# The first normed x by rows and transposes, the odd layer's bias laid out by the host, and the second x.T piece behind the first weights

## The chip, the cores and the metric

The kernel runs on one core of one Trainium2 chip. The metric is the device time of one execution in microseconds (us), lower is better. Five engines work beside each other and meet only at semaphores: TensorE (PE in the profile, with its weight loads as PEld), VectorE (DVE), ScalarE (ACT), GpSimd (POOL) and SyncE (SP). SP, ACT and POOL also issue DMA transfers. Each engine takes its instructions strictly in the order in which the kernel was written out, so an instruction that waits holds up everything behind it on the same engine.

## The reference

Three transformer blocks on 256 tokens of width 1024, all in float32. What matters here is the start of the first block and the neighbourhood attention of the second:

```python
def rmsnorm(x, g):
    y = xf * lax.rsqrt(jnp.mean(xf * xf, axis=-1, keepdims=True) + EPS)
    return y * g

# layer 0 (even)
h = rmsnorm(x, norm_gain[0])
qa, ka, va, qb, kb, vb, qm, gate = split_cols(h @ w_in_even, SPLIT_EVEN)
...
# layer 1 (odd): each of 16 heads, rows of 64 positions
dc = jnp.clip(col[None, :] - col[:, None] + NA_COLS - 1, 0, 2 * NA_COLS - 2)
rpb_cols = rpb[:, :, dc]
s = einsum('bqhd,bikhd->bhqik', qblk, kblk) * scale + bias
s = jnp.where(colmask[:, None, :], s, -jnp.inf)
p = jax.nn.softmax(s)
```

Before them the keys and values of a memory are projected, and after them come a third block (a dilated attention with a gated convolution, a cross attention, a squared-ReLU MLP) and a last norm. The bulk of the work is matrix products of the 256 tokens with about 32 million weights.

## The kernel before

**Numbers.** Every product is made at nearly float32 accuracy from float32r parts. A weight tile `raw` from HBM is split by `split` (lines 430 to 436) into a high part `wh`, written by ACT, and a low part `wl` = raw − wh, written by DVE. The activations have a high and a low part too (`hilo`, or ACT with a scale and DVE's `scalar_tensor_tensor` with the same scale). `mm3` (line 438) then makes high times high, high times low and low times high.

**The plan.** The kernel's methods do not issue instructions. `Plan.record` (line 83) writes each of them down with what it depends on, and `Plan.order` (line 162) runs a list schedule over a simple model of the five engines: at each moment the engine takes, of its ready instructions, the one with the lowest priority number, which is the place in the recording plus `nc.bias` plus `SHIFT`. Transfers are modelled as one bus after the other: 450 ns per issue on SP and ACT, or 1040 ns on POOL, 650 ns of latency, bytes at 358 per ns (line 227), and 950 ns until the data can be used. The sequence that comes out is what all engines' queues get. Semaphores then follow the real dependences between tiles, so a wrong guess of the model costs waiting and nothing else. `either` records an instruction that DVE or ACT may take, whichever is free first in the model; `scaled` and `square_sum` are such.

**Buffers.** `raw` has three buffers, `wh` and `wl` four each. Activations live in 24 equal slots (`slot`). PSUM has four banks under the name `mm` (projections) and four under `at` (attention, transposes).

**The start.** `consts` (line 368) loads the gains, then the first two of x.T's eight 128-row pieces (x.T is prepared by the host), one on SP's and one on ACT's queue, and has PE run 24 warm-up matmuls. `layer_even` (line 1008) begins with the columns of w_in that make q, k and v of the first attention and k and v of the second, 896 columns in all. It does not wait for the norm: `gain_t` (line 519) multiplies x.T by the gain per row into the tile `gh`, and the missing factor 1/rms of each token is applied to the products later. For each of the eight 128-row pieces k, `columns` issues the loads of the weights and `sweep` makes 12 matmuls of 512 and 384 columns into four PSUM banks. Between the loads of weights `load_x` issues the rest of x.T, two pieces at a time. With pieces 6 and 7 come the rows of x itself, from which `sums` and `rstd` get 1/rms (POOL makes the power).

**The first normed x** (lines 1059 to 1067). All later products of this layer need the normed and transposed x, tile `hT`. `spread` (line 534) turns the column r of 1/rms into a row by two diagonal matrices and two float32 matmuls with ones (four PE instructions), and ACT copies the result to SBUF. DVE multiplies x.T by gain and row, eight times 128x256 (tile `xs`), and `hilo` splits this in four pieces of 128x512. The odd layer does the same step in another way: `norm_later` scales x by rows (tile `xn`), and `turns` (line 657) transposes it on PE in 128x128 pieces, with the gain applied while ACT and DVE split the result out of PSUM (tile `mT`).

**The odd layer's bias** (lines 1169 to 1193). For each group of four heads POOL issues two loads of shifted table rows (`rpbraw`), then writes `rpbe`, the column mask minus the table read backwards, with one 128x384 subtraction per head. The bias therefore has the opposite sign, and so have the scores: `heads8` scales q by −0.125, and `softmax` (line 745) adds, takes the minimum, and exponentiates with scale −1.0. The dilated attention of the third block goes through the same code, with its bias in the constants `C_DIL`.

Of the kernel before, what the change touches and what calls it, by code (L numbers as in the profile page):

```python
# [16 lines left out]
P = 128  # L17
S = 256
# [8 lines left out]
C_ID, C_COS, C_SIN, C_DIL, C_COL, C_END = 0, 128, 256, 384, 640, 704  # L27


class Plan:  # L30
# [131 lines left out]
    def order(self, prio):  # L162
# [37 lines left out]
        while len(seq) < n:  # L200
# [19 lines left out]
            if o["bytes"]:  # L220
                if e != "gpsimd":
                    ring[e] = max(ring[e], t) + 450.0
                    avail[e] = (ring[e], i)
                    bus = max(bus, ring[e] + 650.0)
                else:
                    bus = max(bus, end[i] + 650.0)
                bus += o["bytes"] / 358.0
                done = bus + o["after"]
# [79 lines left out]
class Kernel:  # L308
# [59 lines left out]
    def consts(self):  # L368
# [12 lines left out]
        for k, queue in enumerate((nc.sync, nc.scalar)):  # L381
            self.load_x(k, 1, queue)
# [136 lines left out]
    def gain_t(self, src, key, fast=False):  # L519
# [4 lines left out]
        def turn(k):  # L524
            v, g, h, l = src[k // 4][:, k % 4, :], self.gcol(key, k), f(0, k), f(1, k)
            if k == 0 and fast:
# [218 lines left out]
    def softmax(self, sc, bias=None, sink=None, causal=False):  # L745


# [8 lines left out]
        else:  # L756
            for t in range(2):
                nc.vector.tensor_tensor_reduce(out=p[:, t, :n[t]], in0=sc[:, t, :n[t]], in1=bias[t], scale=1.0,
                                               scalar=-NEG if sink is None else NEG, op0=ALU.add,
                                               op1=ALU.min if sink is None else ALU.max, accum_out=nmax[:, t:t + 1])  # L760
# [247 lines left out]
    def layer_even(self):  # L1008
# [5 lines left out]
        def columns(k0, parts, raw=None):  # L1014
# [4 lines left out]
            for j0, j1, d0, d1 in parts:  # L1019
# [17 lines left out]
        for k0 in range(0, KT, 2):  # L1037
            raw = columns(k0, ((0, 1, 0, 512), (0, 2, 512, 768), (0, 2, 768, 896), (1, 2, 0, 512)) if k0 == 0 else
                          ((0, 2, 0, 768), (0, 2, 768, 896)) if k0 < 6 else ((0, 1, 0, 768), (0, 1, 768, 896)))
            if k0 < 6:  # L1040
                self.load_x(k0 + 2, 2, nc.sync)
            else:
# [16 lines left out]
        rb = self.spread(r, self.work("y", [P, S], YB))  # L1059
        hT = Halves(lambda: self.slot([P, 2, 2, S], "hT"))  # L1060
        for c in range(2):
            t = self.slot([P, 4, S], "xs", F32)
            for k in range(4):
                nc.vector.scalar_tensor_tensor(t[:, k, :], self.xT[c][:, k, :], self.gcol("norm0", 4 * c + k), rb,
                                               ALU.mult, ALU.mult)
            for k in (0, 2):
                self.hilo(*hT.pair(4 * c + k), t[:, k:k + 2])
# [70 lines left out]
    def heads8(self, tag, w_in, cq, ck, cv, hT, bias, out, causal=False, before=None):  # L1138

        qs, ks = [], []  # L1140
        for i in range(2):
            ks.append(self.k_stack(self.proj_t(w_in, ck + 256 * i, hT)))
            qs.append(self.q_stack(self.proj_t(w_in, cq + 256 * i, hT), -0.125))
# [11 lines left out]
    def layer_odd(self, ms):  # L1155
# [13 lines left out]
        col = self.c[:, C_COL:C_COL + 64]  # L1169
        rpb = a["rpb_c"]  # L1170

        def biases(gi):
            e = {}

            def bias(h):
                hh = 8 * gi + h
                if h % 4 == 0:
                    raw = self.slot([P, 4, 220], "rpbraw", F32)
                    for rl in range(2):
                        nc.gpsimd.dma_start(raw[rl * 64:(rl + 1) * 64],  # L1180
                                            bass.AP(rpb.tensor, rpb.offset + hh * 465 + 76 + 31 * rl,
                                                    [[1, 64], [465, 4], [1, 220]]))
                    for j in range(4):
                        if j % 2 == 0:
                            e[h + j] = self.slot([P, 2, 6, 64], "rpbe", F32)
                        e[h + j] = e[h + j - j % 2]
                        w = bass.AP(raw.tensor, raw.offset + 220 * j + 218, [list(raw.ap[0]), [-31, 6], [-1, 64]])
                        nc.gpsimd.tensor_tensor(e[h + j][:, j % 2], col.unsqueeze(1).to_broadcast([P, 6, 64]), w,
                                                ALU.subtract)
# [369 lines left out]
```

## Time and profile before

| | |
|---|---|
| time, median of 3 runs | 773.08 us (772.73 to 773.56) |
| the profiled execution's own time | 773.77 us |
| its span, first to last instruction | 771.9 us |
| granted TensorE clock, mean | 0.997 |
| ACT busy | 529.0 us (69%) |
| read from HBM | 134.92 MB, 176 GB/s over the span |
| DMA issued by SP and ACT (q1) | 131.12 MB, 52.7% of 16 engines |
| DMA issued by POOL (q0) | 8.10 MB, 4.8% of 16 engines |
| chain that ended last | PE 82%, ACT 6%, DVE 6%, DMA 3%, issue 2% |

How to read it: "busy" is the time in which an engine has an instruction under way. Matmuls overlap each other, so a busy PE may still be faster or slower than its peak. A row of a group gives the line, engine and operation, the tile written, the tiles read, the shape, the number of instructions, then total busy us and mean ns of one, and last the idle time just before them with what ended it. Almost all instructions have the line 284, since `Plan.issue` emits them; the tiles' names tell them apart. A row of the timeline begins with start and length in us, and merges neighbours of one kind (x2).

### The profile page before, as it was taken

The page shows a single profiled execution, that of the slowest core. Times are in us where ns is not written, and L with a number is a line of the kernel's source. Part 1 is how long each engine was busy: PE and PEld are TensorE (multiplying, and loading weights), DVE is VectorE, ACT ScalarE, POOL GpSimd, SP SyncE. Part 2 cuts the span into 40 slices and gives each one's busy share as a digit, 9 for nine tenths or more (in the row PEclk, how much of TensorE's full clock was granted, in tenths as well). Part 3 has the DMA queues.
Part 4 walks back from the last instruction along what each step waited for, and adds up shares of the span by engine and source line. Part 5 has one row for each costly group of instructions (what it writes and reads, how often), then busy time and mean ns, then how long its engine had stood idle before and what let it go on. Part 6 is the DMA issues. An engine that isn't in the chain of part 4 may idle for free.

```text
span 771.9 us, 11841 instructions
## 1 busy us (share of the span) xinstructions
PE 760.7 (99%) x4370; PEld 662.6 (86%) x4370; DVE 614.3 (80%) x1136; ACT 529.0 (69%) x1034; POOL 66.6 (9%) x98
## 2 busy tenths in 40 slices
PE   9999999999999999999999999999999999999996
PEld 7898888888888888888888898899988888888885
DVE  5999998988779789979998899886677665555655
ACT  5687986976678678757796788466556765555562
POOL 2140010000001511132001000100000000000000
PEclk9999999999999999999999999999999999999998
DMA  8893555445568854765456644356535665656541
GB/s 315 284 268 111 165 183 177 159 165 164 164 211 250 218 188 144 199 197 193 134 191 194 191 163 156 117 165 219 191 110 164 195 188 167 204 177 209 170 163 55
DMA packets 109145, 140.39 MB, mean 182 GB/s; under 512 B 3744, under 2 KB 80736, under 8 KB 109088
## 3 DMA queue, kind: packets, MB, share of 16 engines
q1 hardware_dynamic: 103184, 131.12, 52.7%
q0 software_dynamic: 5472, 8.10, 4.8%
q8 instruction: 34, 0.56, 0.3%
q10 hardware_dynamic: 432, 0.43, 0.2%
q14 instruction: 23, 0.19, 0.1%
HBM read 134.92 MB, written 1.05 MB: 176 GB/s over the span
## 4 chain that ended last, share of the span: by engine, by line
PE 82%; ACT 6%; DVE 6%; DMA 3%; issue 2%; SPq 0%; POOLq 0%; POOL 0%; ACTq 0%; DVEq 0%
PE t_mm L284 61%; PE t_at L284 21%; DVE t_wl L284 2%; DMA t_raw<-in_w_in_even_dram 2%; ACT t_p L284 2%; ACT t_wh L284 2%; ACT t_y L284 1%; DVE t_y L284 1%; DVE t_p L284 1%; DMA t_xT<-in_x_t_dram 0%; ACT t_ph L284 0%; SPq L284 0%; ACT t_sum L284 0%; DVE t_pl L284 0%; DVE t_tanh L284 0%
## 5 line engine op out<-in xcount | busy, mean ns | idle before, releaser
L284 DVE TENSOR_TENSOR t_wl<-t_raw,t_wh 128x1024 fp32r<-128x1024 f32 (+2 forms) x238 | 288.7, 1217 | 69.9 <-ACT t_wh L284 67.2
L284 ACT ACTIVATE t_wh<-t_raw 128x1024 fp32r<-128x1024 f32 (+2 forms) x238 | 249.7, 1054 | 78.7 <-PE t_mm L284 57.4
L284 PE MATMUL t_mm<-t_mT,t_wh 128*128 128x512 f32 x496 | 179.6, 401 | 0.0
L284 PE MATMUL t_mm<-t_mT,t_wl 128*128 128x256 f32 x496 | 131.0, 283 | 0.0
L284 PE MATMUL t_mm<-t_wh,t_yh 128*128 128x512 f32 (+1 forms) x288 | 113.3, 393 | 0.0
L284 PE MATMUL t_mm<-t_wl,t_yh 128*128 128x512 f32 (+1 forms) x288 | 112.3, 390 | 0.0
L284 PE MATMUL t_mm<-t_wh,t_yl 128*128 128x512 f32 (+1 forms) x288 | 111.9, 391 | 0.0
L284 PEld LDWEIGHTS t_mm<-t_mT,t_wh 128*128 128x128 f32 x496 | 91.0, 188 | 13.4
L284 PEld LDWEIGHTS t_mm<-t_mT,t_wl 128*128 128x128 f32 x496 | 93.2, 189 | 6.6
L284 PE MATMUL t_at<-t_mT,t_wh 128*128 128x512 f32 x240 | 86.0, 395 | 0.0
L284 ACT COPY t_sum<-t_mm 128x256 f32<-128x256 f32 x90 | 33.2, 369 | 51.8 <-PE t_mm L284 51.3
L284 PE MATMUL t_mm<-t_wh,t_gh 128*128 128x256 f32 (+2 forms) x256 | 63.8, 333 | 0.0
L284 PEld LDWEIGHTS t_mm<-t_wl,t_yh 128*128 128x128 f32 x288 | 54.2, 188 | 10.7
L284 PEld LDWEIGHTS t_mm<-t_wh,t_yl 128*128 128x128 f32 x288 | 54.1, 188 | 10.6
L284 PEld LDWEIGHTS t_mm<-t_wh,t_yh 128*128 128x128 f32 x288 | 54.1, 188 | 10.3 <-ACT t_yh L284 0.3
L284 PE MATMUL t_at<-t_mT,t_wl 128*128 128x256 f32 x240 | 62.6, 280 | 0.0
L284 ACT ACTIVATE t_p<-t_p,t_st 128x256 f32<-128x256 f32 (+1 forms) x111 | 53.2, 494 | 10.6 <-DVE t_st L284 10.5
L284 PEld LDWEIGHTS t_at<-t_mT,t_wh 128*128 128x128 f32 x240 | 44.5, 188 | 8.3 <-issue 0.2
L284 DVE TENSOR_TENSOR t_sum<-t_mm,t_sum 128x256 f32<-128x256 f32 x90 | 37.9, 422 | 13.9 <-ACT t_sum L284 12.9
L284 PE MATMUL t_mm<-t_hT,t_wh 128*128 128x512 f32 (+1 forms) x160 | 48.3, 356 | 0.0
L284 PEld LDWEIGHTS t_at<-t_mT,t_wl 128*128 128x128 f32 x240 | 45.2, 188 | 3.5
L284 PE MATMUL t_mm<-t_gh,t_wh 128*128 128x512 f32 x128 | 47.3, 404 | 0.0
(189 smaller groups left out, 1371.7 us busy)
## 6 DMA issues: line engine op xcount, KB each, us to landing
t_raw<-in_w_in_odd_dram SPq DMA_DIRECT2D x20, 1024.0 KB, 5.2
t_raw<-in_w_up_dram SPq DMA_DIRECT2D x16, 1024.0 KB, 5.7
t_raw<-in_w_down_dram SPq DMA_DIRECT2D x16, 1024.0 KB, 5.0
t_raw<-in_w_in_dram SPq DMA_DIRECT2D x12, 1024.0 KB, 5.3
t_raw<-in_w_in_even_dram SPq DMA_DIRECT2D x10, 1024.0 KB, 5.1
t_raw<-in_w_mem_kv_dram SPq DMA_DIRECT2D x8, 1024.0 KB, 5.2
t_raw<-in_w_out_even_dram SPq DMA_DIRECT2D x6, 1024.0 KB, 5.2
t_raw<-in_w_out_odd_dram SPq DMA_DIRECT2D x6, 1024.0 KB, 5.9
```

Of the source, the lines that this page charges most:

```text
L284: f(*[self.real(v) for v in args], **{k: self.real(v) for k, v in kwargs.items()})
```

## The change

- The second x.T piece goes from ACT's queue to SP's, behind the first three loads of weights (`columns` now also takes pieces of x.T in its list). Rows 2 and 3 of the weights come as two loads of 384 KB instead of one of 768 KB, with the last 128 columns of both between them.
- In `gain_t` DVE makes the high part of the second x.T piece too, which ACT made before.
- The planner's model moves bytes at 320 per ns instead of 358.
- The first normed x is made as in the odd layer: four scalings of x by rows (`xn`), 16 transposes on PE, and eight halves each on ACT and DVE.
- The host lays out the odd layer's bias per head as 128x384 with mask and sign in it; POOL loads two heads at a time (384 KB) and computes nothing. Scores keep their sign: q is scaled by 0.125, and in `softmax` the sum is negated by the scale of the same DVE instruction. The bias of the dilated attention changes sign in the constants, and the column mask leaves them.

```diff
@@ Plan.order
-                bus += o["bytes"] / 358.0
+                bus += o["bytes"] / 320.0
@@ consts
-        for k, queue in enumerate((nc.sync, nc.scalar)):
-            self.load_x(k, 1, queue)
+        self.load_x(0, 1, nc.sync)
@@ gain_t
-            if k == 0 and fast:
+            if k < 2 and fast:
                 nc.vector.tensor_scalar(h, v, g, None, ALU.mult)
@@ softmax
-                nc.vector.tensor_tensor_reduce(out=p[:, t, :n[t]], in0=sc[:, t, :n[t]], in1=bias[t], scale=1.0,
-                                               scalar=-NEG if sink is None else NEG, op0=ALU.add,
-                                               op1=ALU.min if sink is None else ALU.max, accum_out=nmax[:, t:t + 1])
+                nc.vector.tensor_tensor_reduce(out=p[:, t, :n[t]], in0=sc[:, t, :n[t]], in1=bias[t], scale=1.0 if sink else -1.0,
+                                               scalar=NEG if sink else -NEG, op0=ALU.add,
+                                               op1=ALU.max if sink else ALU.min, accum_out=nmax[:, t:t + 1])
@@ layer_even, columns
-            for j0, j1, d0, d1 in parts:
+            for part in parts:
+                if len(part) == 2:
+                    self.load_x(*part, nc.sync)
+                    continue
+                j0, j1, d0, d1 = part
@@ layer_even, the loop over k0
-            raw = columns(k0, ((0, 1, 0, 512), (0, 2, 512, 768), (0, 2, 768, 896), (1, 2, 0, 512)) if k0 == 0 else
-                          ((0, 2, 0, 768), (0, 2, 768, 896)) if k0 < 6 else ((0, 1, 0, 768), (0, 1, 768, 896)))
-            if k0 < 6:
-                self.load_x(k0 + 2, 2, nc.sync)
-            else:
+            raw = columns(k0, (((0, 1, 0, 512), (0, 2, 512, 768), (0, 2, 768, 896), (1, 1), (1, 2, 0, 512), (2, 2)),
+                               ((0, 1, 0, 768), (0, 2, 768, 896), (1, 2, 0, 768), (4, 2)),
+                               ((0, 2, 0, 768), (0, 2, 768, 896), (6, 2)),
+                               ((0, 1, 0, 768), (0, 1, 768, 896)))[k0 // 2])
+            if k0 == 6:
@@ layer_even, the normed x
-        rb = self.spread(r, self.work("y", [P, S], YB))
-        hT = Halves(lambda: self.slot([P, 2, 2, S], "hT"))
+        halves = [self.slot([P, 2, 512], "xn", F32) for _ in range(2)]
         for c in range(2):
-            t = self.slot([P, 4, S], "xs", F32)
-            for k in range(4):
-                nc.vector.scalar_tensor_tensor(t[:, k, :], self.xT[c][:, k, :], self.gcol("norm0", 4 * c + k), rb,
-                                               ALU.mult, ALU.mult)
-            for k in (0, 2):
-                self.hilo(*hT.pair(4 * c + k), t[:, k:k + 2])
+            for t in range(2):
+                self.scaled(halves[c][:, t, :], self.x[:, t, c * 512:(c + 1) * 512], r[:, t:t + 1])
+        hT = self.turns("n", halves, "norm0")
+        self.flush("n")
@@ heads8
-            qs.append(self.q_stack(self.proj_t(w_in, cq + 256 * i, hT), -0.125))
+            qs.append(self.q_stack(self.proj_t(w_in, cq + 256 * i, hT), 0.125))
@@ layer_odd, bias(h)
-                if h % 4 == 0:
...
+                if h % 2 == 0:
+                    hh = 8 * gi + h
+                    e[h] = self.slot([P, 2, 384], "rpbe", F32)
+                    nc.gpsimd.dma_start(e[h], table[hh:hh + 2].rearrange("h p c -> p h c"))
+                b = e[h - h % 2][:, h % 2]
                 return [b[:, 128:384], b[:, 0:256]]
```

More of the change, by code (lines that the diff above doesn't have):

```diff
@@ L26 @@
 N_GAIN_ROWS = 76
-C_ID, C_COS, C_SIN, C_DIL, C_COL, C_END = 0, 128, 256, 384, 640, 704
+C_ID, C_COS, C_SIN, C_DIL, C_END = 0, 128, 256, 384, 640
 class Plan:
@@ L1168, in layer_odd @@
         self.mem_heads("m", qm, self.mk1, mv, out("m"))
-        col = self.c[:, C_COL:C_COL + 64]
-        rpb = a["rpb_c"]
+        table = a["rpb_c"]
         def biases(gi):
@@ L1175, in bias @@
             def bias(h):
-                hh = 8 * gi + h
-                if h % 4 == 0:
[L1178 to L1189, printed above, removed]
-                b = e[h][:, h % 2].rearrange("p j c -> p (j c)")
+                if h % 2 == 0:
[3 more added lines that the diff above has]
+                b = e[h - h % 2][:, h % 2]
                 return [b[:, 128:384], b[:, 0:256]]
@@ L1494, in constants @@
     mult = ((d >= 0) & (d <= 128)).astype(int) + ((d >= 0) & (d % 4 == 0)) + ((d >= 0) & (d % 16 == 0))
-    c[:, C_DIL:C_DIL + 256] = np.where(mult > 0, -np.log(np.maximum(mult, 1)), -NEG)
-    qc = (np.arange(P) % 64)[:, None]
-    kc = np.arange(64)[None, :]
-    cs = np.clip(qc - 8, 0, 48)
-    c[:, C_COL:C_COL + 64] = np.where((kc >= cs) & (kc < cs + 16), 0.0, -NEG)
+    c[:, C_DIL:C_DIL + 256] = np.where(mult > 0, np.log(np.maximum(mult, 1)), NEG)
     return c
@@ L1526, in transposed, with neighbours @@
     return {n + "_t": np.ascontiguousarray(given[n][0].T) for n in ("x", "mem", "mem_2")}
-def reversed_tables(rpb):
-    return np.ascontiguousarray(rpb.reshape(16, 465)[:, ::-1])
+def neighbours(rpb):
+    rl, qc = (v[:, None, None] for v in divmod(np.arange(P), 64))
+    j, kc = np.arange(6)[None, :, None], np.arange(64)[None, None, :]
+    cs = np.clip(qc - 8, 0, 48)
+    w = rpb.reshape(16, 465)[:, 464 - (294 + 31 * rl + qc - 31 * j - kc)]
+    return np.ascontiguousarray(np.where((kc >= cs) & (kc < cs + 16), w, np.float32(NEG)).reshape(16, P, 384))
 _INS = ["x", "mem", "norm_gain", "mem_norm_gain", "w_in_even", "w_out_even", "q_norm_a", "k_norm_a", "sink_b",
@@ L1547 @@
     given["window"] = window(given["rel_bias"])
-    given["rpb_c"] = reversed_tables(given["rpb_c"])
+    given["rpb_c"] = neighbours(given["rpb_c"])
     given["gains"] = gain_rows(given)
```

## The prediction

> **What bounds the kernel now.** I read the page's first part, then the list of waits for the matmul engine alone, then the busy time by stage.
>
> ```profile
> span 771.9 us, 11841 instructions
> PE 760.7 (99%) x4370; PEld 662.6 (86%) x4370; DVE 614.3 (80%) x1136; ACT 529.0 (69%) x1034; POOL 66.6 (9%) x98
> ```
>
> ```profile
> PE t_at L284 <- DVE t_warm L284: 1.2, 1, 1.2
> PE t_at L284 <- DVE t_p L284: 1.0, 2, 0.6
> PE t_at L284 <- ACT t_wh L284: 0.9, 1, 0.9
> PE t_mm L284 <- DVE t_wl L284: 0.9, 2, 0.6
> PE t_at L284 <- DVE t_pl L284: 0.3, 1, 0.3
> ```
>
> The first fence says that TensorE (PE) does something in all but 11.2 us of the span. The second says who held it up: 1.2 us before the warm-up matmuls, and then 3.1 us in six waits in the whole kernel. The rest, 6.9 us, is the end after the last matmul. So the kernel is bound by the number of matmuls, and an edit pays only by removing matmul time or one of these few waits. Where do they lie?
>
> ```profile
> 0.00:24.00 24.00, 21.61 (x101) 18.71 (x102) 14.45 (x26) 14.58 (x25) 5.34 (x19) 1.00 0.93 314
> 24.00:30.00 6.00, 5.08 (x26) 4.21 (x26) 5.31 (x11) 4.01 (x6) 0.00 (x0) 1.00 0.59 195
> 30.00:52.00 22.00, 21.33 (x174) 20.80 (x173) 21.52 (x53) 19.03 (x39) 10.57 (x13) 1.00 1.06 317
> 52.00:100.00 48.00, 47.64 (x298) 41.01 (x297) 46.67 (x86) 39.00 (x93) 0.28 (x1) 1.00 0.48 155
> 195.00:345.00 150.00, 149.75 (x867) 130.73 (x866) 127.53 (x247) 109.75 (x223) 29.34 (x37) 1.00 0.68 202
> ```
>
> Columns: stage, its length, then busy time of PE, weight loads, DVE, ACT and POOL, granted clock, DMA share, GB/s. All but 0.3 us of the six waits lie before 52 us. There the bound changes: up to 24 us the transfers run at 0.93 of the DMA engines and 314 GB/s; from 30 to 52 us DVE has 0.5 us free in 22. The odd layer (195 to 345 us) leaves PE 0.25 us idle in 150.
>
> The five waits before 52 us, and the transfers in front of three of ACT's conversions, stand in the order of time:
>
> ```profile
> 12.65 0.50 PE L284 MATMUL t_mm<-t_wl,t_gh 128*128 128x512 f32 x1 [0.63 <-DVE t_wl L284]
> 21.77 0.71 PE L284 MATMUL t_at<-t_p,t_ones 128*128 128x128 f32 x4 [0.56 <-DVE t_p L284]
> 28.74 0.51 PE L284 MATMUL t_at<-t_hT,t_wh 128*128 128x256 f32 x2 [0.92 <-ACT t_wh L284]
> 44.02 0.33 PE L284 MATMUL t_at<-t_cst,t_p 128*128 128x128 f32 x1 [0.42 <-DVE t_p L284]
> 51.78 0.39 PE L284 MATMUL t_mm<-t_hT,t_wl 128*128 128x256 f32 x1 [0.25 <-DVE t_wl L284]
> ```
>
> ```profile
> 10.51 1.79 ACT L284 ACTIVATE t_wh<-t_raw 128x896 fp32r<-128x896 f32 x2 [2.04 <-DMA t_raw<-in_w_in_even_dram]
> 15.65 1.80 ACT L284 ACTIVATE t_wh<-t_raw 128x896 fp32r<-128x896 f32 x2 [2.55 <-DMA t_raw<-in_w_in_even_dram]
> 27.63 2.01 ACT L284 ACTIVATE t_wh<-t_raw 128x1024 fp32r<-128x1024 f32 x2 [1.59 <-DMA t_raw<-in_w_in_even_dram]
> ```
>
> A matmul's row is longer than the step to the next one, because they overlap, so a wait costs more than the idle time shown. These rows give the step and the row length:
>
> ```profile
> 195.70 1.69 PE L284 MATMUL t_at<-t_cst,t_xn 128*128 128x128 f32 x14
> 197.15 0.71 PE L284 MATMUL t_mm<-t_wh,t_gh 128*128 128x512 f32 x2
> 197.70 0.40 PE L284 MATMUL t_mm<-t_wl,t_gh 128*128 128x512 f32 x1
> 197.93 0.62 PE L284 MATMUL t_mm<-t_wh,t_gh 128*128 128x512 f32 x2
> ```
>
> One 512-column matmul steps 0.23 us (197.70 to 197.93) but lasts 0.40: 0.17 us is overlap that a wait loses. So the five waits cost about 0.8, 0.7, 1.1, 0.6 and 0.4 us (idle time plus 0.17), 3.6 us in all. That is nearly all there is to win.
>
> **The change part by part.**
>
> **Transfers at the start.** These rows are DVE's low parts of rows 4 and 5 and the first matmul after the ones matmuls:
>
> ```profile
> 16.64 2.09 DVE L284 TENSOR_TENSOR t_wl<-t_raw,t_wh 128x896 fp32r<-128x896 f32 x2 [2.11 <-ACT t_wh L284]
> 22.23 0.47 PE L284 MATMUL t_mm<-t_wl,t_gh 128*128 128x512 f32 x1
> ```
>
> The second x.T piece leaves ACT's queue for SP's and goes behind the first weights, and the 768 KB block of rows 2 and 3 is cut, so that row 2 with its last columns is complete 384 KB earlier. At 314 GB/s that is 1.2 us before the 10.51 at which ACT could start it. The matmul at 12.65 then finds its operand: −0.8. But no byte is saved, so the weights of rows 4 and 5 still come at about 15.65, and their low parts follow on DVE, two in 2.09 us, the first at 17.7. PE needs them earlier by what it gained. The high part's matmuls can go first if the order foresees it. Between nothing and −0.8 I take −0.5. SP gets two more issues (the x.T piece and the second half of the block). The transfers already queued hide them (share 0.93); without that cover the weights come later and the −0.5 is lost, no more. The second piece's high part goes from ACT to DVE, 0.35 us by the row further down, at a time when DVE waits. The first matmul doesn't move, since the warm-up matmuls hold PE until then:
>
> ```profile
> 1.19 5.38 PE L284 MATMUL t_at<-t_warm 128*128 128x256 f32 x24 [1.19 <-DVE t_warm L284]
> ```
>
> **First normed x.** Removed: the diagonal, the four ones matmuls, ACT's copy, and on DVE eight multiplications and four subtractions. Added: four scalings, 16 transposes, eight ACT and eight DVE halves, as the odd layer does already. The two kinds, side by side:
>
> ```profile
> L284 DVE SCALAR_TENSOR_TENSOR t_xs<-t_xT,t_gT,t_y 128x256 f32<-128x256 f32 x8 | 3.3, 479 | 0.0
> L284 DVE TENSOR_TENSOR t_hT<-t_xs,t_hT 128x512 fp32r<-128x512 f32 x4 | 2.6, 686 | 0.9 <-ACT t_hT L284 0.9
> L284 DVE TENSOR_SCALAR t_p<-t_cst,t_rstd 128x128 f32<-128x128 f32 x1 | 0.3, 286 | 0.6 <-POOL t_rstd L284 0.6
> L284 DVE TENSOR_SCALAR t_gh<-t_xT,t_gT 128x256 fp32r<-128x256 f32 x1 | 0.4, 354 | 2.1 <-DMA t_gT<-in_gains_dram 2.1
> ```
>
> ```profile
> L284 DVE SCALAR_TENSOR_TENSOR t_mT<-t_at,t_gT,t_mT 128x256 fp32r<-128x256 f32 x8 | 3.2, 478 | 0.0
> L284 ACT ACTIVATE t_mT<-t_at,t_gT 128x256 fp32r<-128x256 f32 x8 | 3.0, 493 | 0.6 <-PE t_at L284 0.6
> L284 PE MATMUL t_at<-t_cst,t_xn 128*128 128x128 f32 x16 | 2.1, 273 | 0.0
> L284 DVE TENSOR_SCALAR t_xn<-t_x,t_rstd 128x512 f32<-128x512 f32 x3 | 1.3, 483 | 0.8 <-POOL t_rstd L284 0.8
> ```
>
> PE: 14 transposes push the next matmul from 195.70 to 197.15, and the two behind it take 0.55 instead of 0.46: 1.54 us for 14, 0.11 each. 16 of them are +1.76. The four ones matmuls step 0.11 each as well (the four in 21.77 to 22.23): −0.45. Their wait at 21.77 goes: −0.7. DVE: 3.3 + 2.6 + 0.3 = 6.2 us go, 1.3 + 3.2 = 4.5 come, and 0.35 for the x.T piece: 1.35 us less. ACT stays level: eight halves of 3.0 us and one scaling replace four hT conversions, the copy and one diagonal. What could be late next is the first transpose, which waits for x, its squares, POOL's power and the scaling, as the diagonal did; in the odd layer PE did not wait there (the 0.0 of its row).
>
> **The Trainium skill prices this differently.** "TensorE: Matmul & The Clock Gate", Part 4, gives a 128x128 transpose in a kernel's context as about 275 ns; 16 of those would be an estimate of 4.4 us in place of 1.76. The row's mean of 273 ns agrees as a length, but the starts 0.11 us apart say that they overlap.
>
> **The planner's rate, 358 to 320 GB/s.** The order of all queues is fixed by a model of the transfers. By the code's shapes 5.15 MB lie up to the end of x and 7.64 MB up to the first gate weights. The model now has them 1.7 and 2.5 us later, and 320 is near the measured 314. That matters at 28.74: PE's order has a gate matmul ahead of remaining row 7 work, its operand waits for the conversion of 27.63, and ACT sits 1.59 us in front of it while the hT conversions queue behind. With the later arrival the ready work goes first: −1.1, at best that, at worst nothing. The waits of 44.02 and 51.78 are on DVE, which has 1.35 us less to do by then: of 1.0 us I take −0.7. From 52 us on only the order changes; one wait of 0.3 us is left to lose, so I take 0, and ±0.7 for the shuffle, the size of one wait seen here.
>
> **Odd layer.** POOL loses 16 subtractions and eight small loads, and gets eight loads of 384 KB, as big as the window's:
>
> ```profile
> L284 POOL TENSOR_TENSOR t_rpbe<-t_cst,t_rpbraw 128x384 f32<-128x384 f32 x16 | 19.1, 1222 | 16.7 <-DMA t_rpbraw<-in_rpb_c_dram 13.1 <-issue 3.5
> L284 DVE CUSTOM_DVE_ANT_0 t_p<-t_at,t_rpbe 128x256 f32<-128x256 f32 x24 | 9.2, 416 | 0.0
> t_wbias<-in_window_dram POOLq DMA_DIRECT2D x4, 384.0 KB, 6.9
> 256.17 1.26 POOL L284 DMA_DIRECT2D t_rpbraw<-in_rpb_c_dram  x2 [0.21 <-issue]
> ```
>
> DVE never waited for the old bias (0.0), so removing POOL's 19.1 us gives nothing. The loads stay covered while POOL issues each 6.9 us before its use. The sign moves into scale factors: same instructions, nothing. Together 0.
>
> Sum: −0.5 + 1.76 − 0.45 − 0.7 − 1.1 − 0.7 = −1.7 us. The profiled execution took 773.77 us (771.9 of span and 1.9 around it), 0.7 over the median of 773.08; against itself the sum gives 772.1, against the median **771.4**. A measurement here tells 0.2%, 1.55 us, from no change: below 771.53 is faster, above 774.63 slower. My value lies just over that edge.
>
> **The rivals.**
> - **The wait is handed on.** For it: the rows 4 and 5 arrive when they did (15.65), and DVE is full from 30 to 52 us. Then the first term, the 28.74 and the DVE terms give back most: −0.45 − 0.7 + 1.76, and −0.8 of the other 2.3: −0.2, 772.9. Against it: DVE's own load falls.
> - **A transpose holds PE for its whole row.** 16 × 0.273 = 4.37, 2.6 more than my 1.76: +0.9, 774.0. The Trainium skill's rule above says the same. Against it: the 0.11 us steps.
> - **Bias loads come late (slower).** In place of a load and POOL work done ahead, each pair of heads waits for 384 KB. The planner sees 1.04 + 0.65 + 1.23 + 0.95 = 3.9 us by its code, the row says 6.9: 3.0 us too few. It decides where POOL issues less than 6.9 us before DVE's use, and PE stands behind once its score banks are full. Two exposed loads: −1.7 + 6.0 = +4.3, 777.4. Against it: the first raw tables are issued at 256.17, and POOL has 120 of 150 us free, so an early slot is all that is needed.
> - **More than forecast.** All five waits and the small gaps up to 100 us go (the 52 to 100 stage has 0.36 us idle, DVE with 1.3 free): −3.6 + 1.3, and 1.0 for the gaps with their overlap: −3.3, 769.8.
>
> **How the numbers follow.** Forecast 0.48, handed on 0.28, transposes 0.06, late loads 0.10, more 0.08. The forecast's own spread is ±1 us, so six in ten of it fall beyond 0.2% (0.30), the rest inside; with "more" (0.08) and a little of the second rival (0.06) faster has 0.44. Inside: 0.18 + 0.19 + 0.05 = 0.42. Slower: 0.10 and 0.04 from the tails. The range runs from "more" to the transposes' case: 769.6 to 774.2; the late loads lie outside it.
>
> **What would show it.** PE's waits before 52 us: none at the low part of row 2, none on ones matmuls, none on a gate conversion; 16 transposes 0.11 us apart. DVE busy from 24 to 52 us about 1.4 us less. POOL without subtractions, DVE's bias rows still with 0.0 idle. Wrong: new PE waits on t_xn, or DVE waits on the bias's load, or waits after 52 us longer than 0.7 us together.

## The result, and the profile after

The changed kernel takes **775.80 us** (median of 7 runs, 775.37 to 776.05) against 773.56 us for the kernel before beside it: a ratio of 1.0030, 95% interval 1.0021 to 1.0040. It is 2.3 us slower. The forecast was 771.4 us, and the range up to 774.2 us did not hold it. The profiled execution of the changed kernel took 775.94 us.

The page of the changed kernel, its first lines (span; busy time, share, instructions):

```profile
span 774.2 us, 11849 instructions
PE 762.7 (99%) x4382; PEld 664.5 (86%) x4382; DVE 613.0 (79%) x1135; ACT 531.7 (69%) x1036; POOL 49.1 (6%) x82
```

PE has 12 more matmuls, as forecast (16 transposes for four ones matmuls), POOL has lost 17.5 us of work, and the span is 2.3 us longer. The list of PE's waits in the changed kernel (total, times, longest):

```profile
PE t_at L284 <- DVE t_p L284: 1.5, 1, 1.5
PE t_at L284 <- DVE t_warm L284: 1.2, 1, 1.2
PE t_at L284 <- DVE t_pl L284: 0.4, 2, 0.2
PE t_mm L284 <- DVE t_wl L284: 0.4, 1, 0.4
PE t_at L284 <- DVE t_xg L284: 0.3, 1, 0.3
PE t_at L284 <- ACT t_p L284: 0.3, 1, 0.3
```

The wait for `t_wh` is gone, as forecast. So are the two for `t_wl` that stood at 12.65 and 51.78 us, but a new one of 0.43 us for `t_wl` has come at 9.66 us. The largest is now one wait of 1.5 us for DVE's `t_p`, and there is a new one for `t_xg`. Where they stand in time shows the timeline of PE in the changed kernel:

```profile
24.38 0.38 PE L284 MATMUL t_at<-t_cst,t_xn 128*128 128x128 f32 x2
24.51 0.42 PE L284 MATMUL t_mm<-t_wl,t_gh 128*128 128x384 f32 x1
24.77 1.69 PE L284 MATMUL t_at<-t_cst,t_xn 128*128 128x128 f32 x14
26.22 0.66 PE L284 MATMUL t_mm<-t_wh,t_gh 128*128 128x384 f32 x2
...
44.09 0.33 PE L284 MATMUL t_at<-t_cst,t_p 128*128 128x128 f32 x1 [1.50 <-DVE t_p L284]
...
375.01 0.39 PE L284 MATMUL t_at<-t_pl,t_vp 128*128 128x256 f32 x1 [0.20 <-DVE t_pl L284]
...
399.11 1.97 PE L284 MATMUL t_at<-t_cst,t_xg 128*128 128x128 f32 x16 [0.35 <-DVE t_xg L284]
```

The transposes start without a wait and 0.10 us apart (14 in 24.77 to 26.22). The stages of the changed kernel, in the columns of the prediction (busy PE, weight loads, DVE, ACT, POOL; clock; DMA share; GB/s):

```profile
0.00:24.00 24.00, 22.33 (x104) 19.58 (x105) 14.02 (x26) 13.69 (x23) 4.79 (x19) 1.00 0.91 305
24.00:30.00 6.00, 6.00 (x45) 5.71 (x44) 5.57 (x12) 5.85 (x14) 0.00 (x0) 1.00 0.71 233
30.00:52.00 22.00, 20.50 (x170) 20.30 (x170) 20.29 (x49) 18.37 (x34) 10.27 (x12) 1.00 1.05 316
52.00:100.00 48.00, 47.10 (x291) 40.32 (x291) 46.49 (x88) 38.43 (x91) 1.16 (x2) 1.00 0.44 145
...
195.00:345.00 150.00, 149.77 (x865) 130.42 (x864) 126.98 (x244) 111.08 (x223) 15.71 (x25) 1.00 0.67 208
```

Up to 30 us PE is better off (28.33 us busy instead of 26.69). From 30 to 100 us it is worse off (67.60 instead of 68.97). And in 30 to 52 us DVE, full before, has 1.7 us idle now.

**PE's lag.** To see where time goes, the starts of PE's matmuls are compared with a PE that never waits. The lag at a time t is t minus the sum of the usual steps of all matmuls started until then (0.229 us for 512 columns, 0.174 for 384, 0.119 for 256, 0.109 for 128 and about 0.11 for the eight of one column, the common steps in these traces). A wait raises it, work does not. In us:

| kernel | 30 | 52 | 66 | 100 | 345 | 400 | 500 | end | work |
|---|---|---|---|---|---|---|---|---|---|
| before | 7.24 | 8.57 | 9.71 | 10.99 | 12.91 | 13.58 | 14.12 | 14.64 | 750.4 |
| changed | 4.91 | 6.78 | 8.64 | 10.15 | 12.41 | 14.13 | 14.88 | 15.56 | 751.7 |
| changed, old start | 4.99 | 6.33 | 7.12 | 8.16 | 10.24 | 11.87 | 12.59 | 13.12 | 751.7 |
| changed, x first | 5.34 | 6.45 | 7.12 | 8.28 | 10.24 | 11.87 | 12.81 | 13.97 | 751.7 |
| changed, old bias | 5.03 | 6.89 | 8.64 | 10.15 | 12.41 | 13.14 | 13.96 | 13.96 | 751.7 |
| changed, x first, old bias | 5.46 | 6.90 | 7.70 | 8.98 | 10.90 | 11.51 | 12.13 | 12.59 | 751.7 |
| before, new bias alone | 6.41 | 8.21 | 9.48 | 10.76 | 12.57 | 13.87 | 14.81 | 15.49 | 750.4 |

The changed kernel is 2.3 us ahead at 30 us, 1.1 at 66 us, and 0.5 at 345 us. It falls 0.5 behind by 400 us and ends 0.9 behind; with 1.3 us more work that makes the 2.3. So two losses are to be explained, one between 30 and 66 us, one behind 345 us.

Each row is one profiled execution, and executions of one order differ. At 66 us the old start has 7.12, and the new normed x with rate 320 (a run below), whose queues are the same up to there, has 7.70. Of four runs with x first, with the same queues up to there, one has 7.12 and three have 7.70. So a difference of 0.6 us between two rows can be chance.

### The profile page after: what moved, and what is told of

It is laid out like the page before. It is cut to its first block, busy times and chain, and to the rows that moved or that the text cites. A ratio compares the mean times of both kernels' runs of the same rounds, so it can differ in the third digit from the quotient of the medians.

```text
span 774.2 us, 11849 instructions
## 1 busy us (share of the span) xinstructions
PE 762.7 (99%) x4382; PEld 664.5 (86%) x4382; DVE 613.0 (79%) x1135; ACT 531.7 (69%) x1036; POOL 49.1 (6%) x82
## 4 chain that ended last, share of the span: by engine, by line
PE 80%; DVE 8%; ACT 7%; issue 2%; DMA 2%; SPq 0%; POOL 0%; POOLq 0%; DVEq 0%; ACTq 0%
PE t_mm L284 59%; PE t_at L284 21%; DVE t_wl L284 2%; ACT t_p L284 2%; ACT t_wh L284 2%; DMA t_raw<-in_w_in_even_dram 2%; DVE t_p L284 1%; DVE t_y L284 1%; ACT t_y L284 1%; ACT t_ph L284 0%; DVE t_x L284 0%; ACT t_sum L284 0%; DVE t_sum L284 0%; DVE t_pl L284 0%; SPq L284 0%
## 5 line engine op out<-in xcount | busy, mean ns | idle before, releaser
L284 PE MATMUL t_mm<-t_mT,t_wh 128*128 128x512 f32 (+1 forms) x656 | 228.8, 391 | 0.0
L284 PE MATMUL t_mm<-t_mT,t_wl 128*128 128x256 f32 x624 | 166.6, 285 | 0.0
L284 PEld LDWEIGHTS t_mm<-t_mT,t_wh 128*128 128x128 f32 x656 | 119.5, 189 | 15.7
L284 PEld LDWEIGHTS t_mm<-t_mT,t_wl 128*128 128x128 f32 x624 | 117.6, 189 | 7.9
L284 PE MATMUL t_at<-t_mT,t_wh 128*128 128x512 f32 (+1 forms) x320 | 101.3, 369 | 0.0
L284 PE MATMUL t_at<-t_mT,t_wl 128*128 128x256 f32 x280 | 74.1, 281 | 0.0
L284 PEld LDWEIGHTS t_at<-t_mT,t_wh 128*128 128x128 f32 x320 | 57.2, 189 | 8.4 <-issue 0.2
L284 ACT ACTIVATE t_p<-t_p,t_st 128x256 f32<-128x256 f32 (+1 forms) x116 | 55.6, 495 | 8.1 <-DVE t_st L284 7.7
L284 PEld LDWEIGHTS t_at<-t_mT,t_wl 128*128 128x128 f32 x280 | 53.0, 189 | 3.4
L284 PEld LDWEIGHTS t_mm<-t_wh,t_gh 128*128 128x128 f32 x256 | 43.9, 189 | 3.7 <-ACT t_wh L284 0.3
```

What stands on the lines that cost most here:

```text
L284: f(*[self.real(v) for v in args], **{k: self.real(v) for k, v in kwargs.items()})
```

## The experiments

Each ratio is against the kernel before, timed beside it (medians 773.2 to 773.6 us). Most intervals are about 0.1% to either side, 0.7 us.

| run | median us | ratio, 95% interval |
|---|---|---|
| changed kernel | 775.80 | 1.0030 (1.0021 to 1.0040) |
| changed, rate 358 | 777.64 | 1.0064 (1.0050 to 1.0078) |
| changed, old normed x | 776.75 | 1.0043 (1.0031 to 1.0056) |
| changed, old bias | 774.93 | 1.0021 (1.0012 to 1.0029) |
| changed, old start | 773.83 | 1.0003 (0.9994 to 1.0012) |
| before, rate 320 | 775.61 | 1.0026 (1.0014 to 1.0037) |
| before, rate 340 | 774.32 | 1.0010 (1.0001 to 1.0019) |
| before, new normed x | 774.05 | 1.0011 (1.0002 to 1.0020) |
| before, new start | 774.74 | 1.0021 (1.0012 to 1.0030) |
| before, new bias | 774.40 | 1.0012 (1.0003 to 1.0022) |
| before, new normed x and rate 320 | 773.16 | 0.9995 (0.9986 to 1.0004) |
| changed, last sweep first | 775.59 | 1.0029 (1.0018 to 1.0041) |
| changed, last sweep first, old bias | 774.75 | 1.0018 (1.0009 to 1.0027) |
| changed, x first | 774.47 | 1.0016 (1.0007 to 1.0025) |
| changed, x first, old bias | 773.51 | 1.0006 (0.9997 to 1.0015) |
| changed, x first, transposes later | 777.87 | 1.0060 (1.0047 to 1.0073) |
| changed, x first, POOL priced higher | 774.05 | 1.0007 (0.9998 to 1.0016) |

### Each part undone

**The planner's rate back to 358** in the changed kernel.

```diff
-                bus += o["bytes"] / 320.0
+                bus += o["bytes"] / 358.0
```

> The changed kernel with the planner's rate back at 358 bytes per ns, everything else as changed. Theory R (the rate made the order worse behind the start: 1.8 us of new waits after 100 us, most of them at 360 to 400 us): those waits go, the start keeps most of its gain, and the time is 774.0 +- 0.5, about 1.8 below the changed kernel's 775.8. Theory N (the new norm's transposes and what stands behind them are the loss, the rate is neutral): 775.8 +- 0.5. Theory S (any re-planning shuffles the small waits by a us either way): anything from 774 to 777, with new waits at other places than in the changed kernel.

1.0064, against 1.0030, and slower than any of the three theories had it. The timeline of PE in this run shows the wait near 44 us grown:

```profile
46.21 0.33 PE L284 MATMUL t_at<-t_cst,t_p 128*128 128x128 f32 x1 [2.60 <-DVE t_p L284]
```

**The rate of 320 alone**, in the kernel before.

> The kernel before with the planner's rate at 320 and nothing else changed. Theory R: slower, 773.5 + 1.5 = 775.0, with new waits at 360 to 400 us, and the wait of 1.08 us at 28.74 gone. Theory N: 773.5 - 1.1 = 772.4, since the wait at 28.74 goes and nothing comes. Theory S: 772 to 775, with waits at places that neither kernel showed.

1.0026, slower. The first two theories expected the wait for the converted gate weights to go. It grew, from 0.92 to 2.31 us, as PE's and ACT's timelines of this run show:

```profile
30.50 0.58 PE L284 MATMUL t_at<-t_hT,t_wh 128*128 128x256 f32 x1 [2.31 <-ACT t_wh L284]
```

```profile
29.36 1.08 ACT L284 ACTIVATE t_wh<-t_raw 128x1024 fp32r<-128x1024 f32 x1
```

ACT now does other ready work first and has no idle time before this conversion, but PE's order still reaches the gate's matmul before it. What the rate does alone is to clear the waits further up: those at 12.65 and 21.77 us are gone and the lag at 24 us is 4.94, against 5.97 in the kernel before.

So the rate that lies closer to the measured 314 GB/s is no gain by itself: it makes another order, with a larger wait in it. With the new normed x the same 320 is better than 358.

**The old normed x** in the changed kernel (`spread`, `xs` and `hilo` instead of `xn` and `turns`).

> The changed kernel with the first normed x made as before (diagonals, ones matmuls, multiplications of x.T). Theory N: 775.8 - 1.3 (16 transposes out, four ones matmuls back) and the waits behind it gone too: 774.0 or less. Theory R: 774.5 to 775.5, only the 1.3 of transposes, with up to 0.7 of wait back on the ones matmuls. Theory S: 773.5 to 776.5.

1.0043, slower than any of the three theories had it. PE's lag at 40 us is 7.96 instead of 4.99, with three waits for `t_hT` and one for `t_wl` between 28 and 33 us. In this order the new normed x takes 3.0 us of waits away up to 40 us, of which 1.9 are left at 66 us, for 1.3 us of matmuls.

**The old odd bias** in the changed kernel (two raw tables and POOL's subtractions, scores with the other sign).

> The changed kernel with the odd layer's bias, mask and signs as before (POOL subtracts again). The bias's loads are not waited for in the changed kernel, so by theories R and N: 775.8 +- 0.5, the waits at 360 to 400 us unchanged. Theory B (the bias's new times of arrival changed the order from 250 us on and made the waits of 360 to 400 us): those go, 774.7. Theory S: 774.5 to 777.

1.0021, as the theory of the bias had it. Its lag is that of the changed kernel until 345 us, to about 0.1 us, and differs behind: 13.14 instead of 14.13 at 400 us. The waits at 375 and 399 us are absent. So the bias from the host costs about 0.7 to 0.9 us. This pair alone does not show that (the intervals overlap); the other pairs below do.

**The old start** in the changed kernel.

```diff
-        self.load_x(0, 1, nc.sync)
+        for k, queue in enumerate((nc.sync, nc.scalar)):
+            self.load_x(k, 1, queue)
...
-            if k < 2 and fast:
+            if k == 0 and fast:
```

and the old list of pieces in `columns`.

> The changed kernel with the first transfers as before (second x.T piece on ACT's queue, 768 KB block whole, ACT making the second high part). If the start's new order is worth what the changed trace shows up to 24 us against the kernel before (1.06 us less lag of PE, of which 0.7 belongs to the ones matmuls), undoing it costs 0.4 us: 776.2. If what PE gains there is lost at the wait of 44.10 anyway (theory V: that wait ends at a time that DVE sets), 775.8 +- 0.4. Theory S (every new plan moves the small waits): 774.5 to 778.

1.0003: 2.0 us come back, which none of the three theories had. The lag at 24 us is 4.54, and 5.09 in a second execution with the same order, against 4.91 with the new one, so the new start shows no gain even at the start. The lag is still level at 40 us (5.11 and 4.99); the difference comes between 40 and 80 us.

### Each part alone

**Rate 340** in the kernel before.

> The kernel before with the planner's rate at 340 and nothing else changed: a re-planning that adds and removes no instruction. Theory S with the kernel before as a lucky or chosen order: slower, 774.5 to 776.5, with the added waits at places of its own. Theory R (the effect goes with the rate, +2.3 for 38 less as measured at 320): half of it, 774.4. If only 320 is bad: 773.3 +- 0.4.

1.0010, half of what 320 costs. Each rate gives an order of its own, and neither of the two others beats 358 in the kernel before.

**The new bias alone.**

> The kernel before with the odd layer's bias from the host alone. Up to 255 us it should be as before, since nothing recorded ahead of the odd layer's attention differs but the constants and the sign. If the new bias costs by itself, a wait on t_cst,t_xg comes near 398 us and it takes 774.0 to 774.6 us; if the cost only came with the changed kernel's other order, 773.2 to 773.7 us.

1.0012, with the wait on `t_xg` (PE's timeline of this run):

```profile
397.70 1.97 PE L284 MATMUL t_at<-t_cst,t_xg 128*128 128x128 f32 x16 [0.35 <-DVE t_xg L284]
```

Of the bias this says that it costs by itself. But the run says more. Up to the odd layer's attention every queue of this kernel has the same instructions in the same order as the kernel before, one later load of constants being 64 columns narrower. Yet PE and ACT, in their timelines of this run, do not wait where the kernel before did:

```profile
27.82 0.39 PE L284 MATMUL t_at<-t_hT,t_wh 128*128 128x256 f32 x2
```

```profile
26.08 1.99 ACT L284 ACTIVATE t_wh<-t_raw 128x1024 fp32r<-128x1024 f32 x2
```

ACT converts the gate weights at 26.08 us with no idle time, where the kernel before began at 27.63 after 1.59 us of waiting for the transfer. So the wait of 0.92 us at 28.74, on which the forecast put 1.1 us, was that of one execution. And it is not worth much: the lag is 0.83 us smaller at 30 us, and only 0.23 smaller at 66 us. Something else sets the pace in between. Against this execution the changed kernel is ahead by 1.5 us at 30 us, 0.8 at 66 and 0.2 at 345, against the 2.3, 1.1 and 0.5 us of the first.

**The new start alone.**

> The kernel before with the new order of x.T and the cut weights alone. Under theory X the second half of x lands 1.4 us later here too, and the ones matmuls and the first normed x with it: the wait on t_p at 21.8 us grows, or one on t_hT comes behind it; 1 to 2 us slower, 774.5 to 775.5 us. If the new order is a gain by itself (the forecast's -0.5 us), 772.6 to 773.2 us.

1.0021, slower by 1.3 to 1.6 us, as theory X had it: not a gain by itself either. The lag at 24 us is 6.20, against 5.97.

**The new normed x alone**, at rate 358.

> The kernel before with the new normed x alone, the rate left at 358. By the forecast's own terms: +1.76 - 0.45 of PE work, -0.7 for the wait on the ones matmuls, and -1.1 for the gate's wait if the norm rather than the rate removes it: 773 us, within 0.5 us of the kernel before. If rate and norm only pay together, a wait of 1 us or more comes before 66 us and it takes 774.5 us or more.

1.0011, between the two cases. PE has no wait for the gate weights here, without the new rate, but one of 0.68 us for `t_p` at 45.28. **With the rate of 320**, and the old start and bias:

> The kernel before with the new normed x and the rate of 320 alone: old order of x.T and old bias. If the parts add as the runs with one part undone suggest (old start -2.0 us, old bias -0.9 us against the changed kernel's 775.8), it takes 772.9 us and is 0.5 us faster than the kernel before, with no wait over 0.7 us on t_cst,t_p near 44 us and none on t_cst,t_xg near 399 us. If each new order only deals the small waits anew, the parts don't add and it lies anywhere from 773 to 776 us.

0.9995, 773.16 us: level with the kernel before, near the sum of the parts (772.9), and without the two waits named. Rate and norm belong together (1.0026 and 1.0011 alone). It is the best of the variants, and no faster than the kernel before by more than the measurement can tell.

### What the start costs

In the changed kernel DVE ends `t_p`, for which PE waits at 44.09, as late as in the kernel before, though it has less to do. These are the rows in DVE's timelines, of the kernel before and of the changed one:

```profile
43.68 0.29 DVE L284 TENSOR_TENSOR t_p<-t_p,t_tanh 128x128 f32<-128x128 f32 x1
```

```profile
34.01 0.35 DVE L284 SCALAR_TENSOR_TENSOR t_vg<-t_mm,t_rstd,t_vg 128x128 fp32r<-128x128 f32 x1 [0.76 <-ACT t_vg L284]
34.79 0.35 DVE L284 SCALAR_TENSOR_TENSOR t_vg<-t_mm,t_rstd,t_vg 128x128 fp32r<-128x128 f32 x1 [0.43 <-ACT t_tanh L284]
...
43.76 0.28 DVE L284 TENSOR_TENSOR t_p<-t_p,t_tanh 128x128 f32<-128x128 f32 x1
```

DVE is held up at 34 us for `t_vg`. PE's order has 24 matmuls for k of the second attention ahead of the last three of row 7, on whose sums `t_vg` waits. (The first 896 columns hold only v of the second attention; its k is computed here, from the normed x.) The first theory: this order is the cause. **The last sweep first** gives row 7 precedence in the changed kernel.

```diff
             wh, wl = self.split(w)
+            nc.bias = -300 if k == KT - 1 else 0
...
+            nc.bias = 0
```

> The changed kernel with one priority changed: the matmuls of the last weight rows (k = 7) go before other ready matmuls. In the changed kernel 16 groups of kb's matmuls stand ahead of the last three of them, so that v's and k's second half is read by ACT 2.9 us later than it could be, DVE stands idle 1.45 us at 34 us, and the transposes at 44.10 wait 1.66 us for DVE. Theory V (that placing is the cause of the wait): the wait at 44.1 falls under 0.5 us, DVE's idle time from 30 to 36 us goes, the lag of PE at 66 us is 1 us less, the time 774.8. Rival W (the wait is set by DVE's amount of work or by the weights' arrival): the wait stays over 1.2 us, 775.8. Theory S may add or take 1 us behind 66 us.

1.0029: no gain. DVE's idle time at 34 us went, the wait shrank and the lag at 52 us fell to 6.18, but the next wait of the same kind took it back: the lag at 66 us is 8.87. The trace is of an execution 1.15 us slower than the run's median, but the following run shows the same wait of 1.57 us. PE's timeline of this run:

```profile
43.13 0.33 PE L284 MATMUL t_at<-t_cst,t_p 128*128 128x128 f32 x1 [0.32 <-DVE t_p L284]
...
57.15 0.41 PE L284 MATMUL t_at<-t_cst,t_p 128*128 128x128 f32 x2 [1.57 <-DVE t_p L284]
```

The same with the old bias:

> The changed kernel with the priority of the last weight rows and with the odd layer's bias, mask and signs as before. If the two effects add (bias -0.9 as measured with it alone, V -1.0): 773.9 or a little less, level with the kernel before at 773.3. If behind 66 us the plan is dealt anew (theory S): 773 to 776.

1.0018, again no better than without (1.0021). So this order is not the whole cause: with row 7 early and x late, the wait comes back.

The second theory looks further up. DVE's own chain starts with x: squares, `t_rstd`, the scaling `t_xn`, the halves of `t_mT`, then everything up to `t_p`. The changed kernel's queue of SP, in its timeline:

```profile
11.24 0.34 SPq L284 DMA_DIRECT2D t_x<-in_x_dram  x1
11.98 0.96 SPq L284 DMA_DIRECT2D t_raw<-in_w_in_even_dram  x2
12.99 0.44 SPq L284 DMA_DIRECT2D t_x<-in_x_dram  x1
```

Between the halves of x stand the 448 KB of weight row 6, which in the kernel before came behind both halves. The diff moves no load of x: the planner put it there. The squares of x, by the view of the tile (duration; first and last start; the first row is the kernel before, the second the changed one, the third the next run):

```profile
L284 DVE CUSTOM_DVE_ANT_0 t_p<-t_x x2: 684/686/687, 18.7 to 19.3; 128x512 f32<-128x512 f32 x2
```

```profile
L284 DVE CUSTOM_DVE_ANT_0 t_p<-t_x x2: 684/687/690, 19.0 to 21.4; 128x512 f32<-128x512 f32 x2
```

```profile
L284 DVE CUSTOM_DVE_ANT_0 t_p<-t_x x2: 683/684/685, 18.9 to 20.3; 128x512 f32<-128x512 f32 x2
```

**x first**: the changed kernel with one small edit, by which both halves are issued ahead of row 6. The planner then deals the other queues anew from about 19 us on.

```diff
-                    nc.ahead = True
+                    nc.ahead, nc.bias = True, -6
                     nc.sync.dma_start(self.x[:, t, :], a["x"][0, t * P:(t + 1) * P])
-                    nc.ahead = False
+                    nc.ahead, nc.bias = False, 0
```

> The changed kernel, but both halves of x are issued ahead of the weights of rows 6 and 7; in the changed kernel the second half stands behind row 6 (448 KB) and lands at 20.3 us instead of 18.6 to 18.9. Theory X: x's late landing puts DVE's squares, and with them all of DVE's queue up to 44 us, 1.5 us later, and this is the wait of 1.66 us on t_cst,t_p at 44.1 us. Then the squares end near 20.7 instead of 22.0 us, the wait falls under 0.5 us, and the whole takes 774.0 to 774.6 us. Theory D (dealt anew): the wait at 44 goes but as much comes back behind it up to 66 us, and the whole stays at 775.3 to 776.3 us.

1.0016, 774.47 us: 1.1 to 1.3 us of the 2.3 come back, with intervals that just overlap. The wait at 44 us is gone, and less takes its place: a wait of 0.57 us at 50.75, and 0.8 in other executions of this order. At 66 us the lag is 7.12, and 7.70 in those, instead of 8.64. The waits of this run, its row at 50.75, and DVE's row for the same `t_p`, 0.84 us earlier than in the changed kernel:

```profile
PE t_at L284 <- DVE t_warm L284: 1.2, 1, 1.2
PE t_mm L284 <- DVE t_wl L284: 0.6, 1, 0.6
PE t_mm L284 <- ACT t_wh L284: 0.6, 1, 0.6
```

```profile
50.75 0.50 PE L284 MATMUL t_mm<-t_gh,t_wh 128*128 128x512 f32 x1 [0.57 <-ACT t_wh L284]
```

```profile
42.92 0.28 DVE L284 TENSOR_TENSOR t_p<-t_p,t_tanh 128x128 f32<-128x128 f32 x1
```

One thing moves along with x. In PE's timelines the first of row 7's last three matmuls stands behind 24 matmuls for k in the changed kernel, and behind two in x first and the old start:

```profile
31.25 0.34 PE L284 MATMUL t_mm<-t_wh,t_gh 128*128 128x384 f32 x1
```

```profile
28.59 0.34 PE L284 MATMUL t_mm<-t_wh,t_gh 128*128 128x384 f32 x1
```

The first row is the changed kernel, the second x first. So the edit shows what the place of x in the load queue costs with all that the planner derives from it. Row 7 early with x late was run and does not keep the lead. Row 7 late with x early was not run, so how the gain divides between the two stays open.

**x first and the old bias** take out both.

> The changed kernel with the two named causes taken out: x ahead of the weights of rows 6 and 7, and the old odd bias. If they are separate and the whole of the loss, it takes 774.5 - 0.9 = 773.6 us, level with the kernel before, with no wait over 0.5 us on t_cst,t_p near 44 us and none on t_cst,t_xg near 398 us. If waits are only dealt anew, it stays above 774.5 us.

1.0006, 773.51 us: level with the kernel before, as expected (773.6). With x's place and the new bias undone, nothing of the loss is left that can be measured (0.5 us, interval −0.2 to 1.2). Nor is there a gain: this kernel still has 1.3 us more matmul work, so by the ratio about 0.9 us of waits have gone, where the forecast counted 3.0. The old start did somewhat better than x first (1.0003 and 1.0016, the intervals overlap). The lags of these two executions are equal at 400 us, 11.87, and part behind it; that rest was not followed further.

### What the bias costs

DVE does not wait for the bias itself. Its rows and the view of the bias's tile in the changed kernel:

```profile
L284 DVE CUSTOM_DVE_ANT_0 t_p<-t_at,t_rpbe 128x256 f32<-128x256 f32 x32 | 12.4, 414 | 0.0
```

```profile
L284 POOL DMA_DIRECT2D t_rpbe<-in_rpb_c_dram x8: 724/742/752, 257.7 to 354.6; - x8
...
DMA to landing us min/median/max: 3.5/6.5/7.4
```

So the rival of late loads is out. Five pairs of kernels differ in the bias alone: changed and old bias, old start and new normed x with rate 320, last sweep first with both, x first with both, and the kernel before with both. In each the new bias is slower, by 0.0008 to 0.0012 of the ratio, 0.6 to 0.9 us. A single pair would hardly be clear of its intervals; five alike are. In all five the lag grows by 0.6 to 1.0 us more between 345 and 400 us with the new bias.

What the kernels with the new bias have in common (the changed one, the runs with rate 358, old norm, old start, last sweep first, x first, and the bias alone) is PE's wait of about 0.5 us, overlap included, before the transposes of `t_xg` in the third norm. None of those with the old bias has it. With the old bias the same transposes start without a wait, in PE's timeline of the kernel before:

```profile
399.13 1.91 PE L284 MATMUL t_at<-t_cst,t_xg 128*128 128x128 f32 x16
```

Two runs tried whether PE's place for these transposes is the price. **Transposes later**: the changed kernel with x first, and a later priority for these 16.

```diff
+            nc.bias = 150 if key == "mix" else nc.bias
             for j in range(2):
                 ...
                     nc.tensor.transpose(pt[:, j, t * P:(t + 1) * P], ...
+            nc.bias = 0 if key == "mix" else nc.bias
```

> The changed kernel with x first (774.5 us), and the 16 transposes of t_xg given a later place in PE's order, behind some memory matmuls; the bias from the host stays. Theory P: the 0.5 us wait on t_xg, and with it most of the new bias's price, comes from PE's order reaching the transposes before DVE and POOL have made t_xg. Then the wait near 397 us goes and the time falls by 0.5 to 0.9 us, to 773.6 to 774.0 us. Theory L: the price lies in the bias's loads or signs themselves, and 774.3 to 774.8 us stays.

1.0060: the wait on `t_xg` went, but it was too much. The matmuls that need the result now wait, in PE's timeline of this run:

```profile
405.94 0.61 PE L284 MATMUL t_mm<-t_mT,t_wh 128*128 128x512 f32 x1 [2.55 <-DVE t_mT L284]
```

**POOL priced higher**: instead the planner is told that the power in this norm takes 0.9 us more, so that it moves the transposes itself. The power's two rows in POOL's timeline of the changed kernel (spans on POOL are rough), and what DVE does for the first:

```profile
394.72 1.57 POOL L284 TENSOR_TENSOR t_rstd<-t_rstd,t_mhalf 128x2 f32<-128x2 f32 x1 [38.88 <-DVE t_rstd L284]
397.57 0.69 POOL L284 TENSOR_TENSOR t_rstd<-t_rstd,t_mhalf 128x2 f32<-128x2 f32 x1 [1.29 <-DVE t_rstd L284]
```

```profile
396.32 0.16 DVE L284 TENSOR_TENSOR t_rstd<-t_rstd 128x2 f32<-128x2 f32 x1 [0.55 <-POOL t_rstd L284]
```

> As the run before with x first (774.5 us) and the bias from the host, but the planner is told that POOL's power in the third norm takes 0.9 us more (it counts 0.63 us; the trace of the changed kernel has 1.57 us for the first of the two). Only the order behind 385 us changes; the transposes of t_xg come later, and unlike in the run that moved them by hand the planner weighs what waits for them. Theory P (the bias's price is PE's place for these transposes): the 0.5 us wait near 397 us goes, no new one over 0.5 us comes up to 450 us, and it takes 773.6 to 774.0 us. Theory L (the price is in the loads or signs, or lies behind 400 us): 774.3 to 774.8 us.

1.0007, 774.05 us, between the two theories. The wait hardly shrank (0.44 us instead of 0.52 before the transposes, overlap included), so this does not show the price to be that wait.

The traces show one more thing that goes with the bias. The first power of this norm lasts 1.56 to 1.57 us in all nine kernels with the new bias and 1.15 to 1.16 in all nine with the old, and DVE, which makes `t_xg` from it, waits for the power in all nine with the new bias and in none with the old. DVE's order differs there too, so no run separates the longer power from the order. Where the bias's 0.6 to 0.9 us arise is shown to the stage (345 to 400 us for the larger part); which instruction causes it stays open.

## Why the prediction was wrong

- **The terms up to 30 us had the right sum, partly by luck.** −0.5, −0.7 and −1.1 make −2.3, and the lag at 30 us fell by 2.33. But the −0.5 for the transfers did not come from the new order: alone it leaves the lag at 24 us at 6.20, against 5.97 before, while the planner's rate alone brings it to 4.94. And the −1.1 was put on the rate, with which alone PE waits 2.31 us for the gate weights; it also rested on a wait that another execution of the same order does not have.
- **The price of the transposes fits the trace.** 14 of them start within 1.45 us, 0.10 us apart. 12 more matmuls of 128 columns at the step of 0.109 are the 1.31 us by which the work in the table grew, the forecast's +1.76 − 0.45. The price of 275 ns each from the Trainium skill's "TensorE: Matmul & The Clock Gate", Part 4, does not hold as a step here, where it is 0.10 us.
- **The step that failed first: "the waits of 44.02 and 51.78 are on DVE, which has 1.35 us less to do by then: of 1.0 us I take −0.7".** DVE's work did fall, by 1.40 us up to 52 us, 0.97 of it from 24 us on (26.83 to 25.86). But it was counted as if DVE's chain began when it had. The last squares of x began at 21.4 instead of 19.3 us, and the time saved became idle time. `t_p` came at 43.76 instead of 43.68, while PE came 1.0 us earlier (2.3 us less lag, 1.3 us more work): the wait at 44 us grew from 0.42 to 1.50 us of idle time, and the one at 51.78 went. By the forecast's own count (idle time plus 0.17) 1.67 us of waits stand where 1.0 stood: the term was +0.7 in place of −0.7.
- **Why that was missed.** The forecast named x, squares, power and scaling as what could be late next, and looked for the wait at the first transpose only. It also asked of SP's two more issues only whether the weights come late, not what else the planner would place between them. x's second half went behind 448 KB of weights, and x first, with the order that the planner makes of it, gets 1.1 to 1.3 us back.
- **The rival "the wait is handed on" named the right mechanism**, PE's lead taken back where DVE is full from 30 to 52 us. It was priced at 772.9 us, 2.9 too low: it assumed that less work on DVE bounds what is lost, and kept nothing back for a later x.
- **The second step that failed: "From 52 us on only the order changes ... I take 0, and ±0.7" together with "Odd layer ... Together 0".** Alone in the kernel before the bias costs 0.9 us, in the changed one 0.7 to 0.9. Not by late loads, as the rival had it (DVE's 0.0 idle held), but for the larger part between 345 and 400 us, by a cause that stays open. The forecast's own sign of being wrong, more than 0.7 us of waits after 52 us, is there: six waits with 1.5 us of idle time in the changed kernel, against three with 0.5 before.
- **Rate.** The step "with the later arrival the ready work goes first: −1.1, at best that, at worst nothing" had the wrong worst case: alone the rate costs 2.0 us by the ratio (1.0026).
- **A small reading.** The forecast took the last 6.9 us of idle time as the end after the last matmul. That matmul ends at 765.35 of 771.9 us, so the end is 6.5, and 0.4 are gaps too short for the list of waits. Nothing else rests on it.

## What to carry to other kernels

Where one planner orders all queues, parts do not add: here each of the four is slower alone, and two of them together are level. In this kernel a lead won on the engine that bounds it lasted only until a stage where another engine was full, so ask first when that engine's own chain starts: here one load behind another, with the order that followed from it, cost 0.9 to 1.5 us of lag by 66 us. And read after each change the order of the load queue, not only the lines that the diff touches.

## What the runs showed of the hardware

Two executions with the same queues up to that point differ by 1.55 us in when ACT converts the gate weights (27.63 us, after 1.59 us of waiting for the transfer, and 26.08 without waiting), which made a PE wait of 0.92 us in one and none in the other. At 66 us the two were 0.23 us apart, and the four executions with x first up to 0.58 us (7.12 and 7.70). A single wait in one profile can be a chance of the transfers and should not be priced as a property of the kernel before a second profile shows it.
